# Second SwiGLU: up projections as seven block products, with weight sums formed in DRAM

## Chip, cores and metric

One Trainium2 chip, one core. The kernel is timed in device microseconds (us). It runs one decoder layer over 512 tokens. TensorE (PE) multiplies, VectorE (DVE) and ScalarE (ACT) do the elementwise work, GpSimd (POOL) a little of it, and SyncE (SP) issues the transfers.

## The reference, cut to what matters

```python
x = x + 0.5 * swiglu(rms_norm(x, ffn1_norm), ffn1_w_gate, ffn1_w_up, ffn1_w_down)
x = x + token_mixer(rms_norm(x, mix_norm), ...)
x = x + 0.5 * swiglu(rms_norm(x, ffn2_norm), ffn2_w_gate, ffn2_w_up, ffn2_w_down)
return rms_norm(x, final_norm)

def swiglu(x, w_gate, w_up, w_down):
    return (silu(x @ w_gate) * (x @ w_up)) @ w_down
```

x is 512 tokens by 1024 channels (D), the hidden width of each SwiGLU is 2816, and everything is float32. The change concerns `x @ w_gate` and `x @ w_up` of the second SwiGLU.

## The kernel before, in words

**Matmuls.** A float32 operand is split in a high part that TensorE's reduced float32 format holds (fp32r) and a low part, the rest. A product is then three matmuls into one PSUM bank: high weight by high operand, high by low, low by high (`mm3`, L548). The stationary block is 128x128 of weights; what streams is up to 512 columns, here tokens.

**Weights.** `stream` (L490 on) lists all weight blocks of the layer, in order of use, each 128x1024 floats (512 KB). `make` and `weights` (L520, L539) bring the next one: SP's load into a `raw` tile, a cast on ACT to `whi`, a subtraction on DVE to `wlo`. There are four tiles of each.

**Up projections.** The normalized x is turned so that channels lie on partitions; `operand` makes it one pair of tiles xh and xl of 128 x 8 x 512. The hidden width is 22 tiles of 128 (FT). For each, `ffn_up` (L705) takes a block for gate and one for up, makes 24 matmuls of 512 tokens for each (8 channel tiles by 3) into a `ps_gu` bank, and `gated` (L600) forms silu(gate) * up and splits it into hhi (ACT) and hlo (POOL).

**Down projections and output rows.** `rows` (L672) adds up all 8 output banks (4 tiles of 128 tokens by 2 halves of 512 channels, `ps_o`), hidden tile by hidden tile. The last three hidden tiles (TAIL) are done per token tile, so that token tile q is complete while the next is still being multiplied. The mixer's output projection goes through `rows` too, and calls `mixed` (L1111) for each complete token tile: x2 = sum + x, then `renorm` (L660). That one squares x2 (ACT), takes the root and the reciprocal (sb, 128x1), scales x2 to xn, has TensorE transpose xn into a `ps_xt` bank, and writes the two parts into the token columns q of xh and xl. In `channels` (L638), the first two blocks (SPLITS, L635) are multiplied in two pieces, 384 tokens (tiles 0 to 2) and then 128 (tile 3), so that TensorE can begin ahead of the last token tile.

**Order.** Every operation goes through a `Recorder` (L391), and a list scheduler, `Plan` (L146), puts all of them in one fixed order per engine by a cost for each (`cost`, L172) and by how many tiles are free. PSUM has 8 banks, tagged ps. Each engine works through its list in order, and waits on others where data demands it. Nearly all instructions are issued in one line (413, in the changed kernel 428), for they are recorded, so tiles tell what they are. The inputs are arranged on the host by `_layout`.

## Time and profile before

| | us |
|---|---|
| median of 3 runs | 1190.66 (1187.05 to 1193.71) |
| the profiled execution | 1187.19 |
| its span | 1185.4 |
| stage: first up projections | 19 to 250 |
| first down projections | 250 to 364 |
| token mixer | 364 to 766 |
| mixer's output rows | 766 to 813 |
| second up projections | 813 to 1057 |
| second down projections | 1057 to 1179 |

The span goes from the first to the last instruction of the profiled execution; its mean granted TensorE clock was 0.998 of full speed. The stages are read off the chain that ended last, in order of time, whose pieces name the PSUM tile that was being written. In a row of a timeline stand the start in us, the duration of one instruction, the engine, the line, the operation with its tiles (out<-in), the shapes, the count, and in brackets the idle time before it with what ended it. In a group's row stand the busy time in us, the mean ns of one, the idle time before them and its releasers. A row of windows gives the stretch and its length, busy time and instructions of PE, PEld (the load of stationary blocks), DVE, ACT and POOL, then the granted clock, the share of the DMA engines and GB/s.

### The profile page before, as it was taken

How to read it: one execution, taken by the hardware profiler on the slowest of the kernel's cores; microseconds unless marked ns; L12 is line 12 of the kernel's file. 1: busy time of each engine (PE TensorE's matmuls, PEld its weight loads, DVE VectorE, ACT ScalarE, POOL GpSimd, SP SyncE). 2: the span in 40 equal slices, each digit the busy share in tenths (PEclk: the TensorE clock that was granted, in tenths of full speed). 3: DMA queues.
4: the chain of work that ended last, by engine and by line, in shares of the span. 5: the costliest groups of instructions: out<-in, count | busy, mean ns of one | idle time of the engine just before them, and what ended most of it. 6: DMA issues, size and time to landing. Idle time of an engine off the chain costs nothing.

```text
span 1185.4 us, 14680 instructions
## 1 busy us (share of the span) xinstructions
PE 1159.8 (98%) x5944; PEld 951.9 (80%) x5944; DVE 543.4 (46%) x742; ACT 440.4 (37%) x712; POOL 164.2 (14%) x153
## 2 busy tenths in 40 slices
PE   9999999999999999999999999999999999999997
PEld 6888888888888777877777888888888888888886
DVE  7433333332227598985767532726223232322225
ACT  7332323222124865353656423325222232322113
POOL 4211111111100333241100000000111111110000
PEclk9999999999999999999999999999999999999999
DMA  8323222332234022211022232321223323223211
GB/s 310 123 89 133 89 100 96 101 111 92 95 101 142 22 103 100 96 55 54 1 64 80 89 124 89 93 103 72 95 101 107 107 89 106 90 94 102 89 54 71
DMA packets 36068, 113.64 MB, mean 96 GB/s; under 512 B 4128, under 2 KB 5152, under 8 KB 36000
## 3 DMA queue, kind: packets, MB, share of 16 engines
q1 hardware_dynamic: 36000, 112.70, 27.9%
q8 instruction: 46, 0.75, 0.3%
q14 instruction: 22, 0.18, 0.0%
HBM read 108.49 MB, written 4.19 MB: 95 GB/s over the span
## 4 chain that ended last, share of the span: by engine, by line
PE 88%; DVE 6%; ACT 3%; issue 1%; DMA 1%; SPq 0%; POOL 0%; ACTq 0%; DVEq 0%
PE ps_gu L413 40%; PE ps_o L413 23%; PE ps_in L413 16%; PE ps_ob L413 2%; PE ps_oa L413 2%; PE ps_f L413 1%; DVE root L413 1%; PE ps_s L413 1%; DVE xx L413 1%; DVE wlo L413 1%; PE ps_t L413 1%; PE ps_y L413 1%; PE ps_sum L413 0%; DMA raw<-in_gu_dram 0%; ACT sq L413 0%
## 5 line engine op out<-in xcount | busy, mean ns | idle before, releaser
L413 ACT CAST whi<-raw 128x1024 fp32r<-128x1024 f32 (+1 forms) x200 | 201.2, 1008 | 623.2 <-PE ps_gu L413 186.8
L413 DVE TENSOR_TENSOR wlo<-raw,whi 128x1024 fp32r<-128x1024 f32 (+1 forms) x200 | 242.6, 1217 | 359.2 <-ACT whi L413 346.2
L413 PE MATMUL ps_gu<-xh,whi 128*128 128x512 f32 (+1 forms) x720 | 277.5, 387 | 1.6 <-ACT whi L413 1.4
L413 PE MATMUL ps_gu<-xl,whi 128*128 128x512 f32 (+1 forms) x720 | 277.6, 387 | 0.6 <-DVE xl L413 0.5
L413 PE MATMUL ps_gu<-xh,wlo 128*128 128x512 f32 (+1 forms) x720 | 277.4, 386 | 0.0
L413 PEld LDWEIGHTS ps_gu<-xh,whi 128*128 128x128 f32 x720 | 135.3, 188 | 30.2 <-ACT whi L413 3.1
L413 PEld LDWEIGHTS ps_gu<-xl,whi 128*128 128x128 f32 x720 | 135.3, 188 | 28.4 <-DVE xl L413 1.7
L413 PEld LDWEIGHTS ps_gu<-xh,wlo 128*128 128x128 f32 x720 | 135.2, 188 | 26.8
L413 POOL TENSOR_TENSOR hlo<-gg,hhi 128x512 fp32r<-128x512 f32 x44 | 76.8, 1746 | 538.4 <-ACT hhi L413 529.2
L413 PE MATMUL ps_in<-xl,whi 128*128 128x512 f32 (+2 forms) x352 | 136.8, 389 | 1.2 <-DVE xl L413 1.2
L413 PE MATMUL ps_in<-xh,whi 128*128 128x512 f32 (+2 forms) x352 | 136.5, 388 | 0.9 <-ACT xh L413 0.9
L413 PE MATMUL ps_in<-xh,wlo 128*128 128x512 f32 (+2 forms) x352 | 136.6, 388 | 0.0
L413 PE MATMUL ps_o<-whi,hhi 128*128 128x512 f32 x352 | 113.7, 393 | 0.0
L413 PE MATMUL ps_o<-whi,hlo 128*128 128x512 f32 x352 | 113.6, 393 | 0.0
L413 PE MATMUL ps_o<-wlo,hhi 128*128 128x512 f32 x352 | 113.3, 392 | 0.0
L413 DVE TENSOR_TENSOR gg<-gg,ps_gu 128x512 f32<-128x512 f32 x44 | 30.2, 687 | 141.6 <-PE ps_gu L413 141.5
L413 PEld LDWEIGHTS ps_in<-xl,whi 128*128 128x128 f32 x352 | 66.7, 189 | 14.1 <-DVE xl L413 1.5
L413 PEld LDWEIGHTS ps_o<-wlo,hhi 128*128 128x128 f32 x352 | 66.2, 188 | 14.6
L413 PEld LDWEIGHTS ps_o<-whi,hlo 128*128 128x128 f32 x352 | 66.2, 188 | 14.6
L413 PEld LDWEIGHTS ps_in<-xh,whi 128*128 128x128 f32 x352 | 66.5, 189 | 14.1 <-ACT xh L413 1.2
L413 PEld LDWEIGHTS ps_o<-whi,hhi 128*128 128x128 f32 x352 | 66.1, 188 | 14.4
L413 PEld LDWEIGHTS ps_in<-xh,wlo 128*128 128x128 f32 x352 | 66.6, 189 | 12.7
(230 smaller groups left out, 1074.2 us busy)
## 6 DMA issues: line engine op xcount, KB each, us to landing
raw<-in_gu_dram SPq DMA_DIRECT2D x86, 512.0 KB, 3.4
raw<-in_dn_dram SPq DMA_DIRECT2D x44, 512.0 KB, 3.5
raw<-in_win_dram SPq DMA_DIRECT2D x42, 512.0 KB, 3.6
raw<-in_wo_dram SPq DMA_DIRECT2D x8, 512.0 KB, 3.4
x<-in_xT_dram SPq DMA_DIRECT2D x8, 256.0 KB, 4.3
xr<-in_x_dram SPq DMA_DIRECT2D x8, 256.0 KB, 6.2
x1d<-xr SPq DMA_DIRECT2D x8, 256.0 KB, 2.0
raw<-in_wout_dram SPq DMA_DIRECT2D x8, 256.0 KB, 2.5
```

Source lines behind the costliest of these rows:

```text
L413: return getattr(self.plan.engines[e], m)(**k)
```

## The change

**The algorithm.** The hidden tiles are taken in pairs, j = 0 to 10. Pair 0 is multiplied as before, except that all four of its blocks are done in the two pieces of 384 and 128 tokens (`2 * SPLITS`). For each pair j from 1 on, gate and up are each seen as a product of 2 x 2 blocks: two hidden tiles by two halves of D (KH = 4 channel tiles), and two halves of D by two halves of the tokens (256). Instead of eight block products there are seven, in the manner of Strassen and Winograd, on sums and differences of blocks. A block of `gu2` (now laid out as FJ x 4 x 128 x 1024) holds gate and up of one hidden tile and one half of D. A product is 4 x 3 matmuls of 256 columns for gate and as many for up (`block`), and accumulates in one of three pairs of banks, `ps_wx`, `ps_wc` and `ps_ww`. X is copied out between products (q1, u2 and u3, on ACT), and DVE adds the copies to the results. The hidden tile of the second kind comes out with its sign turned, which silu's scale of -1 and a factor of -1 undo.

**Sums of tokens.** Besides xh and xl, four combinations of token halves and halves of D are needed, as high and low parts: tf0 to tf3. `take`, called at the end of `renorm`, makes them from the transposed banks: token tiles 0 and 1 are kept (xt), and with tiles 2 and 3 come t1, t2 and two t34, each cut by `halve` into two casts (ACT) and two subtractions (DVE) of 128 x 2 x 128.

**Sums of weights.** For each pair four sums of blocks are needed: F1 = g2 + g3, F3 = g0 + g2, F2 = g0 + F1, F4 = g1 + F2. They are formed in DRAM, for two pairs at a time, by POOL's transfers of 128x2x1024 floats (1 MB), DRAM to DRAM: four copies, then four that accumulate. This makes 40 transfers. `step_sums` records one after each hidden tile of the first up projections but two (20), one after each row step of the first down projections (19) and one in the mixer's output rows. Each depends on the operation recorded just before it, so none is issued early. In the stream the blocks of a pair then come as g0, g1, F2, F3, F1, g3, F4.

**x2.** Its eight tiles no longer stay until the end: they are written to DRAM (x2d, by SP) in `mixed`, and read back as x3 for the last step.

**The planner** gets a cost for issuing a transfer on POOL (1500 ns), and a rate at which these are thought to land (SOFT).

```diff
+FJ = FT // 2
+KH = KT // 2
...
+    SOFT = 160.0
...
+        if method == "dma_start":
+            return 60.0 if eng == "SP" else 1500.0
...
-                if size:
+                if size and e == "POOL":
+                    soft = max(soft, now + 2000) + size / self.SOFT
+                    o.end = soft + 2000
+                elif size:
...
-    for ft in range(FT):
-        for gu in range(2):
-            stream.append((gu2[ft, :, gu * D:(gu + 1) * D], D))
+    sums = [Part(Slot(dram, [2, P, D], F32, "dram", f"sums{f}_{i}")) for f in range(4) for i in range(FJ // 2)]
+    def summed(f, j):
+        return sums[f * (FJ // 2) + (j - 1) // 2][(j - 1) % 2]
+    for j in range(FJ):
+        for b in range(4) if j == 0 else (0, 1, "F2", "F3", "F1", 3, "F4"):
+            stream.append((gu2[j, b] if isinstance(b, int) else summed(int(b[1]) - 1, j), D))
     for ft in range(FT):
         stream.append((dn2[ft], D))
+    def sum_steps():
+        for i in range(FJ // 2):
+            js = slice(1 + 2 * i, 3 + 2 * i)
+            f1, f2, f3, f4 = (sums[f * (FJ // 2) + i].rearrange("j p d -> p j d") for f in range(4))
+            for to, of in ((f1, 2), (f3, 0), (f2, 0), (f4, 1)):
+                yield G.dma_start(out=to, in_=gu2[js, of].rearrange("j p d -> p j d"))
+            for to, of in ((f1, 3), (f3, 2)):
+                yield G.dma_start(out=to, in_=gu2[js, of].rearrange("j p d -> p j d"), accum_op=ALU.add)
+            yield G.dma_start(out=f2, in_=f1, accum_op=ALU.add)
+            yield G.dma_start(out=f4, in_=f2, accum_op=ALU.add)
+    summing = sum_steps()
+    def step_sums():
+        op = next(summing, None)
+        if op:
+            op.deps.add(op.i - 1)
...
+            if ft > 1:
+                step_sums()
...
+                if gu is None:
+                    wk, wsl = w, sl(kt)
+                else:
+                    wk, wsl = w[kt // KH], slice(gu * S + kt % KH * P, gu * S + kt % KH * P + P)
+                mm3(ps[:, cs_], wk, x, wsl, cs_, kt == 0, kt == KT - 1)
...
-    def renorm(name, q, x3, gain, xg):
+    def renorm(name, q, x3, gain, xg, also=None):
...
+            if also:
+                also(q, hf, ps)
...
+            step_sums()
...
+    def halve(t, form, q):
+        for i in range(2):
+            hi, lo = (x[i][:, :, sl(q)].keyed(q) for x in form)
+            part = t.rearrange("p (k t) -> p k t", t=P)[:, 2 * i:2 * i + 2]
+            A.copy(out=hi, in_=part)
+            V.tensor_tensor(out=lo, in0=part, in1=hi.bitcast(F32), op=ALU.subtract)
...
+        def take(q, hf, ps):
+            flat = ps.rearrange("p k t -> p (k t)")
+            if q < 2:
+                t = t2k("xt")
+                A.copy(out=t, in_=flat)
+                kept[q, hf] = t
+                return
+            q -= 2
+            if hf == 0:
+                t1 = t2k("t1")
+                V.tensor_tensor(out=t1, in0=kept[q, 0], in1=flat, op=ALU.subtract)
+                halve(t1, forms[0], q)
+                kept[q] = t1
+                return
+            t2 = t2k("t2")
+            V.scalar_tensor_tensor(out=t2, in0=flat, scalar=-1.0, in1=kept[q], op0=ALU.mult, op1=ALU.subtract)
+            halve(t2, forms[1], q)
+            for i in range(2):
+                t = t2k("t34")
+                V.scalar_tensor_tensor(out=t, in0=t2, scalar=-1.0, in1=kept[q, i], op0=ALU.mult, op1=ALU.subtract)
+                halve(t, forms[2 + i], q)
...
+    def block(ps, w, gu, x, start):
+        for k in range(KH):
+            wsl = slice(gu * S + k * P, gu * S + (k + 1) * P)
+            whi, wlo = w
+            xhi, xlo = x(k)
+            T.matmul(ps, lhsT=whi[:, wsl], rhs=xhi, start=start and k == 0, stop=False, skip_group_check=True)
+            T.matmul(ps, lhsT=whi[:, wsl], rhs=xlo, start=False, stop=False, skip_group_check=True)
+            T.matmul(ps, lhsT=wlo[:, wsl], rhs=xhi, start=False, stop=k == KH - 1, skip_group_check=True)
...
+    def ffn_up(xg, forms):
+        split_left[0] = 2 * SPLITS
         hs = []
-        for ft in range(FT):
+        for cb in range(2):
+            ws = [weights(1), weights(1)]
             pair = [psum("ps_gu") for _ in range(2)]
             for gu in range(2):
-                channels(xg, pair[gu], weights())
+                channels(xg, pair[gu], ws, gu)
             hs.append(gated(pair, None))
+        H = 2 * P
+        def plain(kb, tb):
+            return lambda k: [t[:, kb * KH + k, tb * H:tb * H + H].keyed([(2 * tb, kb), (2 * tb + 1, kb)]) for t in xg]
+        def formed(i):
+            return lambda k: [t[k // 2][:, k % 2] for t in forms[i]]
+        for j in range(1, FJ):
+            def both(ps, x, start):
+                w = weights()
+                for gu in range(2):
+                    block(ps[gu], w, gu, x, start)
+            def aside(name):
+                t = t2k(name)
+                ps = [t[:, gu * H:gu * H + H].keyed(gu) for gu in range(2)]
+                for gu in range(2):
+                    A.copy(out=ps[gu], in_=X[gu])
+                return ps
+            X, C, W = ([psum(n)[:, 0:H] for _ in range(2)] for n in ("ps_wx", "ps_wc", "ps_ww"))
+            top = [t2k(n) for n in ("gg", "uu")]
+            low_ = [t2k(n) for n in ("gg", "uu")]
+            both(X, plain(0, 0), True)
+            q1 = aside("q1")
+            both(C, plain(1, 0), True)
+            for gu in range(2):
+                V.tensor_tensor(out=top[gu][:, 0:H].keyed(0), in0=C[gu], in1=q1[gu], op=ALU.add)
+            both(X, formed(1), False)
+            u2 = aside("u2")
+            both(X, formed(2), False)
+            u3 = aside("u3")
+            both(W, formed(0), True)
+            for gu in range(2):
+                V.tensor_tensor(out=low_[gu][:, H:S].keyed(1), in0=W[gu], in1=u3[gu], op=ALU.add)
+            both(X, formed(3), False)
+            A.activation(out=low_[0][:, 0:H].keyed(0), in_=X[0], func=AF.Silu, scale=-1.0)
+            A.copy(out=low_[1][:, 0:H].keyed(0), in_=X[1])
+            A.activation(out=low_[0][:, H:S].keyed(1), in_=low_[0][:, H:S].keyed(1), func=AF.Silu, scale=-1.0)
+            V.scalar_tensor_tensor(out=low_[0], in0=low_[0], scalar=-1.0, in1=low_[1], op0=ALU.mult, op1=ALU.mult)
+            both(W, plain(1, 1), False)
+            for gu in range(2):
+                V.tensor_tensor(out=top[gu][:, H:S].keyed(1), in0=W[gu], in1=u2[gu], op=ALU.add)
+            A.activation(out=top[0], in_=top[0], func=AF.Silu)
+            V.tensor_tensor(out=top[0], in0=top[0], in1=top[1], op=ALU.mult)
+            hs.append(finished(top[0]))
+            hs.append(finished(low_[0]))
...
+            Q.dma_start(out=x2d.keyed(2 * q + hf)[2 * q + hf], in_=x2)
+        renorm("sb", q, res[q], gain, xg, take)
...
-    o["gu2"] = gu(w["ffn2_w_gate"], w["ffn2_w_up"])
+    g2 = np.stack([w["ffn2_w_gate"], w["ffn2_w_up"]]).reshape(2, 2, KH, P, FJ, 2, P)
+    o["gu2"] = g2.transpose(4, 5, 1, 3, 0, 2, 6).reshape(FJ, 4, P, D)
```

**Where it moves instructions.** The first place is DVE between the mixer's output rows and the second up projections. sb2 and sb3 are the reciprocal roots of token tiles 2 and 3, xn their normalized tiles. Before, x2_5064 and x2_5076 are the two halves of token tile 3, and the first row is the second xn of token tile 2:

```order
L413 SCALAR_TENSOR_TENSOR xn_6429<-x2_5046,sb2_6384,gff2_4948 128x512
L413 TENSOR_TENSOR x2_5064<-ps_o_6158,x2_5064 128x512
L413 TENSOR_TENSOR wlo_6446<-raw_6212,whi_6431 128x1024
L413 TENSOR_TENSOR xl_6365<-ps_xt_6434,xh_6358 128x4x128
L413 TENSOR_TENSOR xl_6365<-ps_xt_6441,xh_6358 128x4x128
L413 TENSOR_TENSOR x2_5076<-ps_o_6160,x2_5076 128x512
L413 TENSOR_TENSOR wlo_6475<-raw_6242,whi_6461 128x1024
L413 TENSOR_TENSOR sb3_6451<-sb3_6451 128x1
L413 TENSOR_TENSOR wlo_6487<-raw_6272,whi_6468 128x1024
L413 RECIPROCAL sb3_6451<-sb3_6451 128x1
L413 SCALAR_TENSOR_TENSOR xn_6503<-x2_5064,sb3_6451,gff2_4930 128x512
L413 SCALAR_TENSOR_TENSOR xn_6508<-x2_5076,sb3_6451,gff2_4948 128x512
```

In the changed kernel x2_5123 and x2_5135 are the halves of token tile 3, xt the kept tiles 0 and 1:

```order
L428 TENSOR_TENSOR sb2_6450<-sb2_6450 128x1
L428 TENSOR_TENSOR x2_5135<-ps_o_6219,x2_5135 128x512
L428 RECIPROCAL sb2_6450<-sb2_6450 128x1
L428 SCALAR_TENSOR_TENSOR xn_6516<-x2_5099,sb2_6450,gff2_4989 128x512
L428 SCALAR_TENSOR_TENSOR xn_6522<-x2_5105,sb2_6450,gff2_5007 128x512
L428 TENSOR_TENSOR sb3_6504<-sb3_6504 128x1
L428 TENSOR_TENSOR wlo_6530<-raw_6272,whi_6511 128x1024
L428 TENSOR_TENSOR xl_6434<-ps_xt_6524,xh_6422 128x4x128
L428 TENSOR_TENSOR t1_6553<-xt_6429,ps_xt_6524 128x512
```

A few rows further on, still in the changed kernel, the last sums of this token tile and the start of token tile 3's:

```order
L428 SCALAR_TENSOR_TENSOR t34_6579<-t2_6568,xt_6429 128x512
L428 TENSOR_TENSOR tf1l_6587<-t2_6568,tf1h_6576 128x2x128
L428 TENSOR_TENSOR tf1l_6593<-t2_6568,tf1h_6582 128x2x128
L428 TENSOR_TENSOR tf2l_6599<-t34_6579,tf2h_6590 128x2x128
L428 TENSOR_TENSOR tf2l_6603<-t34_6579,tf2h_6595 128x2x128
L428 SCALAR_TENSOR_TENSOR t34_6606<-t2_6568,xt_6438 128x512
L428 RECIPROCAL sb3_6504<-sb3_6504 128x1
L428 TENSOR_TENSOR wlo_6613<-raw_6302,whi_6520 128x1024
L428 TENSOR_TENSOR tf3l_6626<-t34_6606,tf3h_6616 128x2x128
L428 TENSOR_TENSOR tf3l_6632<-t34_6606,tf3h_6619 128x2x128
L428 SCALAR_TENSOR_TENSOR xn_6636<-x2_5123,sb3_6504,gff2_4989 128x512
L428 SCALAR_TENSOR_TENSOR xn_6642<-x2_5135,sb3_6504,gff2_5007 128x512
```

Before, the reciprocal and the xn of token tile 2 stood ahead of tile 3's x2; now they stand behind the last of it. Between token tile 2's xn and token tile 3's now stand two wlo, two xl, the four sums t1, t2 and t34, and eight halves of tf0 to tf3 (two of each of them at this place).

The second place is POOL in the mixer, where bh is the product that the mixer's key step needs. Before:

```order
L412 MEMSET xx_2301 64x4x64
L412 MEMSET xx_2331 64x4x64
L413 TENSOR_TENSOR bh_2841<-iclr_2764,ilam_2829 128x512
L413 TENSOR_TENSOR bh_2853<-iclr_2777,ilam_2845 128x512
L413 TENSOR_TENSOR bh_2864<-iclr_2812,ilam_2856 128x512
L413 TENSOR_TENSOR bh_2878<-iclr_2823,ilam_2867 128x512
```

Now (sums0 to sums3 are F1 to F4, and the last number of the name the two pairs):

```order
L428 DMA sums1_4_2351<-in_gu2_dram 128x2x1024
L427 MEMSET xx_2362 64x4x64
L427 MEMSET xx_2381 64x4x64
L428 DMA sums3_4_2387<-in_gu2_dram 128x2x1024
L428 DMA sums0_3_1998<-in_gu2_dram 128x2x1024
L428 DMA sums2_3_2034<-in_gu2_dram 128x2x1024
L428 DMA sums3_2_1841<-sums1_2_1754 128x2x1024
L428 TENSOR_TENSOR bh_2895<-iclr_2817,ilam_2882 128x512
L428 TENSOR_TENSOR bh_2907<-iclr_2830,ilam_2899 128x512
```

34 of the 40 transfers now stand ahead of the first bh. The last of them, sums3_2<-sums1_2, accumulates the F2 of its pairs, and so it waits for that one's landing, which is the 27th transfer in POOL's order.

More of the change, by code (lines that the diff above doesn't have):

```diff
@@ L130, in __init__ @@
         self.users, self.state, self.made, self.place, self.held = [], {}, None, None, {}
-        self.psum = tag == "ps"
+        self.psum, self.dram = tag == "ps", tag == "dram"
     def real(self):
         if self.made is None:
-            self.made = self.pool.tile(list(self.shape), self.dt, tag=f"{self.tag}{self.place}" if self.tag else self.name, name=self.name)
+            self.made = self.pool.tile(list(self.shape), self.dt, tag=f"{self.tag}{self.place}" if self.place is not None else self.name, name=self.name)
         return self.made
@@ L199, in add @@
         op = Op()
-        op.port = sum(isinstance(p.tile, Slot) and not p.tile.psum and p.free > 1 for p in parts)
+        op.port = sum(isinstance(p.tile, Slot) and not p.tile.psum and not p.tile.dram and p.free > 1 for p in parts)
         op.i, op.ways, op.table, op.outs = len(self.ops), ways, table, []
@@ L253, in order @@
         free_at = {e: 0.0 for e in names}
-        table, dma, dge, port = None, 0.0, 0.0, 0.0
+        table, dma, dge, soft, port = None, 0.0, 0.0, 0.0, 0.0
         front, now, done = 0, 0.0, 0
@@ L407, in record @@
                     size = 4 * int(np.prod((out if isinstance(out, Part) else kw["in_"]).arr.shape))
+                    if isinstance(out, Part) and out.tile.dram:
+                        size *= 2
                 def emit(e=e, m=m):
@@ L636, in layer_kernel, with channels @@
     split_left = [0]
-    def channels(xg, ps, w):
+    def channels(xg, ps, w, gu=None):
         cols = [(0, NQ)]
@@ L647, in channels @@
                 x = [t[:, kt].keyed([(q, kt // 4) for q in range(a, b)]) for t in xg]
-                mm3(ps[:, cs_], w, x, sl(kt), cs_, kt == 0, kt == KT - 1)
+                if gu is None:
[3 more added lines that the diff above has]
+                mm3(ps[:, cs_], wk, x, wsl, cs_, kt == 0, kt == KT - 1)
     def rstd_of(name, x3):
@@ L703, in halves, with token_sums, tiles @@
         return out_
-    def ffn_up(xg):
-        split_left[0] = SPLITS
+    def halve(t, form, q):
[4 more added lines that the diff above has]
+            V.tensor_tensor(out=lo, in0=part, in1=hi.bitcast(F32), op=ALU.subtract)
+    def token_sums():
+        def tiles(name, where):
+            if where is None:
+                return [t2k(name, [P, 2, 2 * P], F32R) for _ in range(2)]
+            t = Part(Slot(inv, [P, KH, 2 * P], F32R, "inv", name))
+            return [t[:, 0:2], t[:, 2:4]]
+        forms = [[tiles(f"tf{i}{part}", inv if i == 0 else None) for part in "hl"] for i in range(4)]
+        kept = {}
+        def take(q, hf, ps):
[19 more added lines that the diff above has]
+                halve(t, forms[2 + i], q)
+        return forms, take
@@ L707, in ffn_up, with finished @@
+    def finished(gg):
+        hi = t2k("hhi", dt=F32R)
+        lo = t2k("hlo", dt=F32R)
+        A.copy(out=hi, in_=gg)
+        G.tensor_tensor(out=lo, in0=gg, in1=hi.bitcast(F32), op=ALU.subtract)
+        return hi, lo
+    def ffn_up(xg, forms):
+        split_left[0] = 2 * SPLITS
         hs = []
-        for ft in range(FT):
+        for cb in range(2):
+            ws = [weights(1), weights(1)]
             pair = [psum("ps_gu") for _ in range(2)]
             for gu in range(2):
-                channels(xg, pair[gu], weights())
+                channels(xg, pair[gu], ws, gu)
@@ L749, in layer_kernel @@
     xg = operand()
-    x1d = Part(Slot(dram, [2 * NQ, P, S], F32, None, "x1d"))
+    x1d = Part(Slot(dram, [2 * NQ, P, S], F32, "dram", "x1d"))
     def first_done(q, ps):
@@ L1109, in layer_kernel @@
     xg = operand()
+    x2d = Part(Slot(dram, [2 * NQ, P, S], F32, "dram", "x2d"))
+    forms, take = token_sums()
     def mixed(q, ps):
@@ L1114, in mixed @@
             V.tensor_tensor(out=x2, in0=ps[hf], in1=x2, op=ALU.add)
-        renorm("sb", q, res[q], gain, xg)
+            Q.dma_start(out=x2d.keyed(2 * q + hf)[2 * q + hf], in_=x2)
+        renorm("sb", q, res[q], gain, xg, take)
     rows(ms, mixed)
-    hs = ffn_up(xg)
+    hs = ffn_up(xg, forms)
     gain = halves("gfin", gfin)
+    res = []
+    for q in range(NQ):
+        res.append([])
+        for hf in range(2):
+            t_ = t2k("x3")
+            Q.dma_start(out=t_, in_=x2d.keyed(2 * q + hf)[2 * q + hf])
+            res[q].append(t_)
     def last(q, ps):
```

## Prediction

> **What bounds the kernel now.** I read the page first: the share of each engine, then the chain that ended last.
>
> ```profile
> span 1185.4 us, 14680 instructions
> ...
> PE 1159.8 (98%) x5944; PEld 951.9 (80%) x5944; DVE 543.4 (46%) x742; ACT 440.4 (37%) x712; POOL 164.2 (14%) x153
> ...
> PE 88%; DVE 6%; ACT 3%; issue 1%; DMA 1%; SPq 0%; POOL 0%; ACTq 0%; DVEq 0%
> ```
>
> TensorE is the bound nearly everywhere, and DVE, ACT and POOL have room. So the change is worth what it takes off TensorE, less every place where TensorE has to stand. Next I read the chain of waits in order of time where the second feed-forward runs:
>
> ```profile
> 813.90 4.80 PE ps_gu L413 x26
> 819.76 237.22 PE ps_gu L413 x1075
> 1056.98 121.52 PE ps_o L413 x528
> ```
>
> From 813.9 to 1057.0 the chain never leaves TensorE: no load, cast or subtraction holds it, and the down projection follows without a gap. Only the up projections are rewritten, so only these 243 us can shrink. The pace inside them is best read from POOL's timeline, where one subtraction (hlo) ends each tile of 128 hidden channels:
>
> ```profile
> 840.90 1.78 POOL L413 TENSOR_TENSOR hlo<-gg,hhi 128x512 fp32r<-128x512 f32 x1 [9.05 <-ACT hhi L413]
> ...
> 1058.63 1.65 POOL L413 TENSOR_TENSOR hlo<-gg,hhi 128x512 fp32r<-128x512 f32 x1 [9.20 <-ACT hhi L413]
> ```
>
> They are the second and the last of 22, so 20 tiles lie between: 217.73 / 20 = 10.89 us for 48 matmuls of 512 columns, 226.8 ns each.
>
> **Part 1, the matmuls.** For two tiles of hidden channels the old code needs 96 matmuls of 512 columns, the new one 7 products x 2 (gate, up) x 4 x 3 = 168 of 256 columns: in columns 7/8, in instructions 7/4. So the price of a 256-column matmul decides, and this trace has none. It has 384 and 128 columns, in the two blocks that are split by token columns; TensorE's timeline, starts in us:
>
> ```profile
> 815.25 0.33 PE L413 MATMUL ps_gu<-xh,wlo 128*128 128x384 f32 x1
> ...
> 817.85 0.33 PE L413 MATMUL ps_gu<-xh,wlo 128*128 128x384 f32 x1
> ...
> 825.68 0.27 PE L413 MATMUL ps_gu<-xl,whi 128*128 128x128 f32 x1
> ...
> 828.14 0.28 PE L413 MATMUL ps_gu<-xh,wlo 128*128 128x128 f32 x1
> ```
>
> The first two are 15 matmuls apart: 173.3 ns for 384 columns. The last two are 22 apart: 111.8 ns for 128. From 384 to 512 columns the price rises 0.418 ns a column, and that line leaves 12.8 ns per matmul which does not depend on width; it would give 66 ns at 128, so there something else, of 111.8 ns, sets the pace: the load of the stationary block, one for each matmul. At 256 columns the line gives 119.8 ns, just above this floor. The floor bounds it below, 111.8 ns. Above, the straight chord from 128 to 384 columns bounds it: 142.6 ns. I take the line, plus a little, because four of the seven products stream operands out of the small shared tiles, not out of the one big operand. What that does is seen in two pieces of the chain:
>
> ```profile
> 700.32 43.55 PE ps_in L413 x192
> 743.87 22.24 PE ps_ob L413 x96
> ```
>
> The first streams the big operand, 226.8 ns; the second small tiles, 231.7 ns. Half of the 4.9 ns for 4 of 7 products is 1.4 ns: 121 ns.
>
> Before, 42 unsplit blocks x 24 x 226.8 ns = 228.6 us. Now two of these become split ones, each 24 x (173.3 + 111.8) ns = 6.84 us, together 13.7 us; the other 40 become 1680 matmuls x 121 ns = 203.3 us. Sum -11.6 us. The bounds give -27.1 us (111.8 ns) and +24.7 us (142.6 ns); the work breaks even at 127.9 ns.
>
> The Trainium skill speaks to this price (TensorE: Matmul & The Clock Gate, Back-to-back issue gap): a warm matmul of N columns takes N/2.4 + 2.5 ns, by estimate 109.2 ns at 256 columns and 215.8 ns at 512; this trace does not agree, with 226.8 ns at 512. By that estimate the sum of this part would be -31.5 us, and the rows, which hold 111.8 ns even at 128 columns, decide against it.
>
> **Part 2, the start of the up projections.** The new code makes four more operand forms from the normalized tokens, on DVE and ACT, between the last output product of the mixer and the first up projection. Both orders of DVE stand above, with the change. What the operations cost is in the groups with each shape apart, and in DVE's timeline:
>
> ```profile
> L413 DVE TENSOR_TENSOR wlo<-raw,whi 128x1024 fp32r<-128x1024 f32 x184 | 234.1, 1275 | 353.3 <-ACT whi L413 346.0
> L413 ACT CAST whi<-raw 128x1024 fp32r<-128x1024 f32 x184 | 193.3, 1052 | 611.4 <-PE ps_gu L413 186.8 <-PE ps_o L413 182.0 <-issue 145.1
> ...
> L413 DVE TENSOR_TENSOR wlo<-raw,whi 128x256 fp32r<-128x256 f32 x8 | 3.1, 416 | 0.2 <-ACT whi L413 0.2
> ...
> L413 ACT COPY rhs<-ps_x 128x256 f32<-128x256 f32 x8 | 2.6, 375 | 0.9 <-PE ps_x L413 0.9
> ```
> ```profile
> 814.36 0.68 DVE L413 TENSOR_TENSOR x<-ps_o,x 128x512 f32<-128x512 f32 x1
> ...
> 817.29 0.15 DVE L413 RECIPROCAL sb<-sb 128x1 f32<-128x1 f32 x1
> 817.48 1.41 DVE L413 SCALAR_TENSOR_TENSOR xn<-x,sb,gff 128x512 f32<-128x512 f32 x2
> ```
>
> TensorE waits today for almost none of it; its own timeline:
>
> ```profile
> 813.90 0.45 PE L413 MATMUL ps_gu<-xl,whi 128*128 128x384 f32 x1 [0.49 <-DVE xl L413]
> ```
>
> Now token tile 2 is normalized only after the sum of tile 3 (x2, then the reciprocal, then xn), so behind the end E of the last output product come 0.17 us of signal, 0.68, 0.15 and 0.70 us until its transposes can start, then a cast and a subtraction: TensorE starts the up projection at about E + 3.6 us. Before, it stood 0.5 us there, and its transposes lay among the output products (0.7 us that only move): 2.5 us more. Second, between tile 2's xn and tile 3's, DVE now has 2 wlo (2 x 1.28 us), 2 xl and 4 sums over 512 elements (6 x 0.68), and 8 halves (8 x 0.42): 10.0 us. Tile 2's xn end at E + 2.4, so tile 3's first one ends at about E + 13.1. TensorE's cover is 45 matmuls x 173.3 ns = 7.8 us, to E + 11.4; 1.7 us and one more short wait make 1.9 us. Bounds for both: 0.5 us (the waits of today) and 7 us (no cover from the second split pair). Third, the clock. After the same renormalization ahead of the mixer it drops; the row of that stretch (its third column from the right is the granted clock), and TensorE's timeline in it:
>
> ```profile
> 364.00:382.00 18.00, 15.90 (x77) 13.57 (x76) 14.92 (x26) 9.80 (x22) 0.00 (x0) 0.91 0.48 158
> ```
> ```profile
> 378.08 0.53 PE L413 MATMUL ps_in<-xl,whi 128*128 128x384 f32 x1
> ...
> 380.96 0.52 PE L413 MATMUL ps_in<-xl,whi 128*128 128x384 f32 x1
> ```
>
> Nine starts in 2.88 us are 320 ns each instead of 173: behind 2.1 us of TensorE idleness (18.00 - 15.90), ten matmuls lost 1.5 us. With some 3 us idle at the new start I charge the same 1.5 us (0 to 1.7, one such stretch at half pace). The Trainium skill (TensorE: Matmul & The Clock Gate, Part 1: The HAM clock gate) says that half clock follows an idle window of about 3.4 us; this trace shows it behind 2.1 us, in pieces. By the Trainium skill this term would be nil, and the sum 1.5 us better.
>
> **Part 3, the other work of a step.** One j (two tiles) lasts 168 x 121 ns = 20.3 us. ACT has 7 casts and six copies of 128x256 out of PSUM, DVE 7 subtractions and a few sums. By the rows of part 2 the seven are 7.4 and 8.9 us, the rest some 5 and 4: about 12.5 us on each engine, under 20.3. The tight spot is the third product: bank X is copied out (u2) and at once written again. Gate and up halves alternate, so each copy has 12 matmuls, 1.45 us, to hide 0.38 us and two signals, and the ACT order puts at most one cast of 1.05 us in front: it fits, barely. I charge 0.5 us over ten steps (0 to 10 x 0.6 us, if each step were late by half a cast). The stream now brings 512 KB per 2.9 us.
>
> **Part 4, the sums in DRAM.** POOL issues 40 transfers of 1 MB, the first behind the third hlo, and in the mixer its products (bh) stand behind 34 of them; the last of those waits for the landing of the 27th. POOL's timeline, the issues by kind and the queue:
>
> ```profile
> 44.53 1.79 POOL L413 TENSOR_TENSOR hlo<-gg,hhi 128x512 fp32r<-128x512 f32 x1 [2.40 <-ACT hhi L413]
> ...
> 403.21 5.04 POOL L413 TENSOR_TENSOR bh<-iclr,ilam 128x512 f32<-128x512 f32 x4 [87.13 <-ACT ilam L413]
> ```
> ```profile
> raw<-in_gu_dram SPq DMA_DIRECT2D x86, 512.0 KB, 3.4
> ...
> x1d<-xr SPq DMA_DIRECT2D x8, 256.0 KB, 2.0
> ```
> ```profile
> q1 hardware_dynamic: 36000, 112.70, 27.9%
> ```
>
> 27 landings between 46.3 and 403.2 us allow 13.2 us for each. No row shows such a transfer. Lower bound: 112.70 MB in 27.9% of 1185.4 us is 341 GB/s, 3.1 us for 1 MB counted once. Upper bound: read and write at the landing times of the rows, 2 x 3.4 + 4 x 2.0 = 14.8 us, and 6.8 us more where the target is read too: 18.2 us on average. Queued transfers go by rate, so I count read, write and target at 341 GB/s: 6.2 and 9.2 us, mean 7.7 us, and 11 us with the weights taking 30% of the engines. That is under 13.2, so no wait. Cost: two issues among the key products, 0.7 us (0, in POOL's gaps, to 3.6, two hlo lengths). The write and reload of x2 and the loads behind it on SP's queue I cost at nothing: five blocks are loaded ahead.
>
> **Sum**, against the profiled execution's 1187.19 us (span 1185.4 and 1.8 around it): -11.6 + 2.5 + 1.9 + 1.5 + 0.5 + 0.7 = -4.5 us. The median, 1190.66 us, lies 3.5 us above that execution; on it the forecast is **1186.2 us**.
>
> **The rivals.** (a) *Half the columns, half the price.* If the 12.8 ns belong to the switch between PSUM banks of 512 columns and not to each matmul, 256 columns cost 113.4 ns: 1680 x 7.6 ns = 12.8 us better, 1173.4 us. For it: 113.4 is above the floor. Against: 384 columns pay them too. The Trainium skill's 2.5 ns, above, makes the same claim. (b) *POOL blocked, slower.* If a transfer takes longer than 13.2 us on average, POOL stands in front of bh by 27 times the excess; DVE's in-order queue waits for bh with the wlo of the next weights behind it, and TensorE runs dry after three prepared blocks (16 us). It decides from 13.8 us on; at 15 us it costs 48.6 - 16 = 32 us: 1219 us. For it: the upper bound, and accumulating must read its target. Against: the rate. (c) *Loads of the stationary block collide with matmuls of nearly equal length*: 131.6 ns, halfway to the chord, is 17.8 us worse, 1204 us. Against: 111.8 ns were kept with far shorter matmuls. (d) *Weights late*: 512 KB in 2.9 us is 181 GB/s, just over half of 341, four buffers deep; unlikely, some 20 us.
>
> **How the numbers follow.** Forecast 0.62, with a range of its own of 1179 to 1193; (a) 0.14, (b) 0.13, (c) 0.08, (d) 0.03. A measurement of this kernel tells about 0.5% from no change, 6 us: 1184.7 to 1196.6. The forecast's 4.5 us lie inside that and near its edge: 0.23 faster, 0.37 same, 0.02 slower. With (a) faster, (b) slower but for 0.01, (c) and (d) slower: faster 0.37, same 0.38, slower 0.25. The range 1172 to 1204 leaves out most of (b) and the outer ends of (a) and (c), under 2 in 10.
>
> **What would show it.** Right: starts of ps_wx, ps_wc and ps_ww 121 ns apart; two waits of TensorE ahead of ps_gu (about 3 and 2 us) and a dip of the clock there; no idleness within a step; bh on POOL near 403 us with ACT as its releaser. Wrong: bh released by a transfer and late (b); a pace under 115 or over 128 ns (a, c); waits of ps_w tiles on whi or on a load (d).

## The result, and the profile after

| | before | after |
|---|---|---|
| median of 13 runs each, us | 1189.39 | 1182.71 |
| ratio after to before, 95% interval | | 0.9939 [0.9922, 0.9957] |
| the profiled execution, us | 1187.19 | 1180.79 |
| first down projections' end to output rows (mixer) | 402.08 | 407.84 |
| output rows to the end of the second up projections | 290.87 | 278.42 |

The changed kernel is 6.7 us faster by the medians, where 4.5 us were forecast. All times here are of executions in the chip's faster state; one of the six of early_one, below, ran at a mean granted clock of 0.616, took 1718.13 us and is left out. The page of the profile after, its span and its engines:

```profile
span 1179.0 us, 16693 instructions
...
PE 1150.9 (98%) x6712; PEld 978.5 (83%) x6712; DVE 617.6 (52%) x862; ACT 500.8 (42%) x839; POOL 189.9 (16%) x190
```

TensorE is as full as before, only with less to do. The shares hide where the time went; the chain in order of time shows it. First two pieces of the kernel before, start and length in us, that the prediction did not need:

```profile
364.03 3.94 PE ps_o L413 x17
...
766.11 36.65 PE ps_o L413 x159
```

And the chain of the changed kernel:

```profile
364.66 3.93 PE ps_o L428 x17
...
772.50 36.58 PE ps_o L428 x159
...
822.59 7.90 PE ps_gu L428 x44
...
850.41 2.93 PE ps_wx L428 x24
853.33 2.88 PE ps_wc L428 x24
...
1050.92 121.81 PE ps_o L428 x528
```

Taking the two executions apart at these pieces: up to 364 us the new one is 0.63 us later. From there to the output rows it takes 407.84 instead of 402.08 us, 5.76 us **lost**. From the output rows to the second down projections it takes 278.42 instead of 290.87 us, 12.45 us **won**. The rest is 0.34 us shorter. Together -6.40 us, the difference of the two profiled executions. So the up projections gained more than twice what I had reckoned, and the mixer, whose code did not change, gave nearly half of it back.

**The up projections.** The stretch of the ten steps, in the row of windows:

```profile
850.40:1050.90 200.50, 200.50 (x1682) 200.50 (x1681) 125.94 (x150) 116.21 (x189) 28.52 (x19) 1.00 0.60 197
```

TensorE does not stand for one moment, at full clock. From the first ps_wx to the down projections there are 200.5 us for 1680 matmuls: 119.3 ns each. DVE works 63% of the stretch and ACT 58%; 197 GB/s are moved, and no engine's wait in this stretch ends with a load. Then TensorE's timeline at the start:

```profile
820.21 1.22 PE L428 MATMUL ps_xt<-cs,xn 128*128 128x128 f32 x8 [1.73 <-ACT sq L428]
821.56 0.96 PE L428 MATMUL ps_gu<-xh,whi 128*128 128x384 f32 x4
822.59 0.44 PE L428 MATMUL ps_gu<-xl,whi 128*128 128x384 f32 x1
...
832.83 0.22 PE L428 MATMUL ps_gu<-xl,whi 128*128 128x128 f32 x1
```

One wait of 1.73 us, as forecast: tile 2's xn stand behind the x2 of tile 3. The bracket names ACT, but in DVE's timeline these xn start at 819.32 us, right behind that x2 and the reciprocal, and the transposes follow at 820.21. The second wait, for token tile 3, is not there: the pieces of 384 tokens go on up to 832.8, 14.5 us behind the end E of the last output product (818.3 us), because eight of the second pair's follow those of the first before the pieces of token tile 3 go on.

**POOL.** POOL's timeline with the last transfer ahead of bh, and bh; then the page's issues by kind, whose last column is the median time to landing:

```profile
341.47 1.13 POOL L428 DMA_DIRECT2D sums<-sums  x1 [7.98 <-issue]
402.29 5.04 POOL L428 TENSOR_TENSOR bh<-iclr,ilam 128x512 f32<-128x512 f32 x4 [59.69 <-ACT ilam L428]
```

```profile
sums<-in_gu_dram POOLq DMA_DIRECT2D x30, 1024.0 KB, 8.3
...
sums<-sums POOLq DMA_DIRECT2D x10, 1024.0 KB, 9.5
```

POOL has issued the last of them 60 us before bh, and stands then for ACT's ilam, as before. From issue to landing they take 8.3 and 9.5 us in the median, where 13.2 us were left for each.

**The mixer.** What is new in its waits is in the list of TensorE's waits between 458 and 535 us, of before and of after:

```profile
PE ps_i L413 <- DVE un L413: 1.4, 1, 1.4
```
```profile
PE ps_i L428 <- DVE un L428: 3.0, 1, 3.0
```

un is a transpose on DVE that ps_i needs. Behind the longer wait the granted clock (third column from the right) falls for 10 us; windows of the changed kernel:

```profile
500.00:502.00 2.00, 0.10 (x1) 0.00 (x0) 2.00 (x2) 0.80 (x4) 0.73 (x3) 1.00 0.00 0
...
504.00:506.00 2.00, 2.00 (x6) 1.50 (x5) 1.93 (x6) 1.51 (x7) 1.83 (x2) 0.50 0.00 0
...
510.00:512.00 2.00, 2.00 (x49) 1.28 (x46) 0.00 (x0) 1.32 (x5) 0.00 (x0) 0.50 1.08 215
```

These windows point at what the loss consists of, and the windows of the whole mixer settle it for the two executions, first before, then after:

```profile
364.03:766.11 402.08, 386.63 (x2505) 314.03 (x2505) 273.40 (x433) 203.91 (x393) 64.85 (x78) 1.00 0.24 79
```
```profile
364.66:772.50 407.84, 392.34 (x2505) 316.68 (x2505) 275.89 (x439) 202.90 (x390) 67.21 (x81) 0.98 0.33 93
```

TensorE stands idle for 15.45 us in the one and 15.50 us in the other. Of the 5.76 us, 5.71 are busy time of the same 2505 matmuls. So in these two executions the longer wait for un is made up elsewhere, and what is lost is clock: in windows of 2 us it lies under 1.00 before the change from 376 to 382 us only, and after it from 410 to 414, 502 to 514 and 620 to 626 us. Busy time times the missing share of the clock, added up over these windows, is 1.7 us before and 7.9 us after (an estimate from the rows). The profiled execution of before had a mean clock of 0.998, near the top of its executions (0.987 to 0.999 in the 28 beside early), so part of the 5.76 us can be its luck; the experiments ask what remains in the medians.

The mixer's code is the same, but its order is not. Six of POOL's transfers stand in it, each costed at 1500 ns by the planner, which lays out everything anew around them: between the last ps_t and the first ps_i it puts 167 matmuls of the input projection (ps_in) where it put 236 before.

### The profile page after: what moved, and what is told of

Its sections match the earlier page's. It is cut to its first block, busy times and chain, and to the rows that moved or that the text cites. A ratio compares the mean times of both kernels' runs of the same rounds, so it can differ in the third digit from the quotient of the medians.

```text
span 1179.0 us, 16693 instructions
## 1 busy us (share of the span) xinstructions
PE 1150.9 (98%) x6712; PEld 978.5 (83%) x6712; DVE 617.6 (52%) x862; ACT 500.8 (42%) x839; POOL 189.9 (16%) x190
## 4 chain that ended last, share of the span: by engine, by line
PE 89%; DVE 5%; ACT 4%; issue 1%; DMA 1%; SPq 0%; DVEq 0%; ACTq 0%
PE ps_o L428 24%; PE ps_gu L428 22%; PE ps_in L428 16%; PE ps_wx L428 10%; PE ps_ww L428 5%; PE ps_wc L428 2%; PE ps_ob L428 2%; PE ps_oa L428 2%; PE ps_f L428 1%; DVE root L428 1%; PE ps_s L428 1%; PE ps_t L428 1%; DVE wlo L428 1%; PE ps_y L428 1%; PE ps_pq L428 1%
## 5 line engine op out<-in xcount | busy, mean ns | idle before, releaser
L428 ACT CAST whi<-raw 128x1024 fp32r<-128x1024 f32 (+1 forms) x230 | 232.6, 1013 | 547.0 <-PE ps_o L428 179.0
L428 DVE TENSOR_TENSOR wlo<-raw,whi 128x1024 fp32r<-128x1024 f32 (+1 forms) x230 | 274.9, 1198 | 342.0 <-ACT whi L428 334.8
L428 PE MATMUL ps_gu<-xh,whi 128*128 128x512 f32 (+2 forms) x416 | 155.6, 377 | 3.4 <-ACT whi L428 3.0
L428 PE MATMUL ps_gu<-xl,whi 128*128 128x512 f32 (+2 forms) x416 | 156.4, 377 | 0.2
L428 PE MATMUL ps_gu<-xh,wlo 128*128 128x512 f32 (+2 forms) x416 | 156.1, 377 | 0.0
L428 POOL TENSOR_TENSOR hlo<-gg,hhi 128x512 fp32r<-128x512 f32 x44 | 70.7, 1608 | 517.2 <-ACT hhi L428 509.2
L428 PE MATMUL ps_o<-wlo,hhi 128*128 128x512 f32 x352 | 113.4, 392 | 0.0
L428 PEld LDWEIGHTS ps_gu<-xh,whi 128*128 128x128 f32 x416 | 78.0, 188 | 19.1 <-ACT whi L428 4.3
L428 PEld LDWEIGHTS ps_gu<-xl,whi 128*128 128x128 f32 x416 | 78.2, 188 | 15.1 <-DVE xl L428 1.3
L428 PEld LDWEIGHTS ps_gu<-xh,wlo 128*128 128x128 f32 x416 | 78.2, 188 | 13.5
L428 PEld LDWEIGHTS ps_in<-xl,whi 128*128 128x128 f32 x352 | 66.9, 190 | 14.4 <-DVE xl L428 1.5
L428 PEld LDWEIGHTS ps_in<-xh,whi 128*128 128x128 f32 x352 | 66.8, 190 | 14.4 <-ACT xh L428 1.2
L428 PEld LDWEIGHTS ps_o<-whi,hhi 128*128 128x128 f32 x352 | 66.0, 188 | 14.5
L428 DVE TENSOR_TENSOR gg<-gg,ps_gu 128x512 f32<-128x512 f32 x24 | 16.4, 687 | 67.7 <-PE ps_gu L428 67.6
```

The costliest lines, as they stand in the source:

```text
L428: return getattr(self.plan.engines[e], m)(**k)
```

## The experiments

Theory 1: the mixer's loss comes from the planner's order, and in particular from the wait for un and the clock behind it. Theory 2: it comes from the transfers themselves. Theory 3: it is the chance of one execution. All results; the mixer, and TensorE's idle time in it, are measured in the profiled execution, by the same two pieces of the chain as above. Each ratio is to executions of the kernel before that ran beside that experiment, with medians from 1188.4 to 1189.4 us:

| kernel | median us | ratio to before | mixer us | TensorE idle in it, us |
|---|---|---|---|---|
| before | 1189.4 | | 402.08 | 15.45 |
| after | 1182.7 | 0.9939 [0.9922, 0.9957] | 407.84 | 15.50 |
| early | 1178.4 | 0.9902 [0.9873, 0.9931] | 402.61 | 15.88 |
| tiny_sums | 1181.9 | 0.9932 [0.9912, 0.9952] | 411.18 | 15.54 |
| before_sums | 1194.1 | 1.0035 [1.0016, 1.0053] | 407.63 | 15.55 |
| keep_warm | 1182.7 | 0.9940 [0.9919, 0.9961] | 413.47 | 15.59 |
| slow_un | 1191.6 | 1.0017 [1.0001, 1.0033] | 410.99 | 17.29 |
| before_256 | 1199.8 | 1.0076 [1.0046, 1.0106] | 404.08 | 15.83 |
| no_sums | 1177.2 | 0.9897 [0.9873, 0.9921] | 402.82 | 16.02 |
| early_one | 1176.0 | 0.9883 [0.9860, 0.9906] | 403.57 | 15.14 |
| soft_180 | 1176.6 | 0.9894 [0.9863, 0.9924] | 405.44 | 15.02 |
| soft_200 | 1177.1 | 0.9900 [0.9870, 0.9931] | 402.08 | 14.50 |

The profiled executions of tiny_sums, keep_warm and slow_un were 3 to 5 us above their medians and that of soft_200 2.4 us below, so a single mixer time can be off by as much. The idle time is nearly the same in all but slow_un: what differs between the mixers here is mostly TensorE's pace.

### early: all transfers ahead of the mixer

```diff
-    SOFT = 160.0
+    SOFT = 300.0
```

> The planner is told that POOL's transfers land nearly twice as fast (SOFT 300 instead of 160), so that 39 of the 40 stand ahead of bh instead of 34; TensorE's and DVE's orders in the mixer are then those of the kernel before. Theory 1 (order): the mixer's extra 5.7 us (402.1 before, 407.9 after) come from the order that the planner made around the six transfers that stood in it: TensorE stood 3.0 us in one piece ahead of un, and the clock went to 0.5 for 10 us. Then the mixer takes 402 us, the clock stays at 1.00 there, and the time falls from 1182.7 to about 1177 us, 0.990 of before. Theory 2 (traffic: the six issues and their bytes in the mixer delay it): also about 402 us here. Theory 3 (chance of one execution): mixer unchanged near 408 or scattered, 1182 us. If a transfer takes longer than the 9.1 us that are left for each (39 landings from 47 to 402 us), POOL stands ahead of bh and the mixer gets longer by up to 39 times the excess.

The mixer took 402.61 us and the ratio is 0.9902, as theories 1 and 2 said. Its chain and POOL's bh:

```profile
365.98 3.95 PE ps_o L428 x17
...
768.59 36.65 PE ps_o L428 x159
```
```profile
387.57 1.15 POOL L428 DMA_DIRECT2D sums<-sums  x1 [10.11 <-PE ps_in L428]
403.65 5.05 POOL L428 TENSOR_TENSOR bh<-iclr,ilam 128x512 f32<-128x512 f32 x4 [14.94 <-issue]
```

bh comes 37.7 us behind the first piece, 39.2 us before the change: even with 39 transfers ahead POOL is on time. The clock was not at 1.00 throughout, which I had expected it to be: 0.93 and 0.64 stand in the windows from 408 to 412 and to 416 us, where the changed kernel has a dip as well.

### tiny_sums: the same order, next to no bytes

```diff
+TINY = 8
...
-            f1, f2, f3, f4 = (sums[f * (FJ // 2) + i].rearrange("j p d -> p j d") for f in range(4))
+            f1, f2, f3, f4 = (sums[f * (FJ // 2) + i].rearrange("j p d -> p j d")[:, :, 0:TINY] for f in range(4))
```

> The planner's order is that of the changed kernel, but each of POOL's 40 transfers carries 8 floats a row instead of 1024 (8 KB instead of 1 MB), and the stream takes plain blocks in place of the sums: what is left out are the sums of weights, so the hidden tiles come out with other numbers, while every instruction of the other engines stays. Theory 1 (order): mixer 408 us as in the changed kernel, with the 3.0 us wait ahead of un and the half clock behind it; 1182 us. Theory 2 (traffic): mixer back to about 402 us, 1177 us. Both: second up projections unchanged at 232 us.

```profile
364.12 3.95 PE ps_o L431 x17
...
775.30 36.58 PE ps_o L431 x159
```
```profile
PE ps_i L431 <- DVE un L431: 3.0, 1, 3.0
```

Its chain and its wait, above: with 1/128 of the bytes in the changed kernel's order the loss is all there: 1181.9 us, the wait of 3.0 us too. The bytes of theory 2 fall; the issues on POOL are still in this order, and soft_180 and soft_200, below, speak to them.

### before_sums: the transfers alone, in the kernel before

```diff
+            if ft > 1:
+                step_sums()
...
+            step_sums()
```

(with `sum_steps` and the planner's costs of the changed kernel, reading `gu2` as it lay before; nobody reads the sums)

> The kernel before with the 40 transfers of 1 MB added at the same places, their results never read. The planner then gives the mixer the order of the changed kernel. Theory 1 and theory 2: mixer 408 instead of 402 us and the second up projections unchanged at 244 us, so 5 to 6 us slower than before, ratio 1.005. Theory 3: ratio 1.000. If the transfers slowed the first feed-forward too (its weights come through the same DMA engines), its 345 us from first to last matmul would grow; I expect no growth.

```profile
364.57 3.94 PE ps_o L421 x17
...
772.20 36.58 PE ps_o L421 x159
```

1.0035, some 4 us slower by the ratio and 5 by the medians, and a mixer of 407.63 us: the price of the transfers' place in the order without any of the gain. The loss comes in a third program with this order, in its median too, so theory 3 falls. From the first to the last matmul of the first feed-forward nothing grew: its up projections had 221.93 us in the piece of 979 matmuls, as before.

### keep_warm: two matmuls that fill the wait for un

```diff
+        ps = psum("ps_keep")
+        for _ in range(KEEP):
+            T.matmul(ps, lhsT=one, rhs=uo.rearrange("p s i -> p (s i)")[:, 0:S], start=True, stop=True)
```

> The changed kernel with two matmuls of 512 float32 columns added, which read uo and whose result nobody uses; they stand where TensorE waited 3.0 us for un, and cover some 1.7 us of it. Nothing else of the computation changes. Theory 1, its second half (it is the clock that costs, not the wait): the wait is cut in two of under 1.5 us, the clock stays at 1.00 in this stretch, and the mixer takes about 4 us less, 404 us; the time about 1179 us. If the wait alone costs, and the clock is no matter: mixer still about 408 us, as the added matmuls end before un does.

```profile
502.35 2.81 PE L429 MATMUL ps_keep<-uo,one 128*128 128x512 f32 x4 [2.27 <-DVE uo L429]
```
```profile
504.00:506.00 2.00, 2.00 (x19) 0.82 (x17) 1.93 (x6) 1.94 (x8) 1.66 (x3) 0.50 0.00 0
506.00:508.00 2.00, 1.52 (x25) 0.91 (x21) 1.87 (x7) 0.53 (x3) 0.00 (x0) 0.82 0.00 0
508.00:510.00 2.00, 2.00 (x24) 1.33 (x22) 1.29 (x5) 1.90 (x5) 0.00 (x0) 1.00 0.00 0
```

A miss. The low clock lasted some 3.5 us instead of 10, yet the median is that of the changed kernel. The 2.27 us ahead of the filler were enough to lower the clock, and the filler itself took 2.81 us of TensorE, much of it at that clock. What was saved went into it, so this run's median doesn't tell clock and wait apart. Its mixer of 413.47 us also holds the filler and another dip, of half clock from 636 to 650 us, far behind it.

### slow_un: the wait lengthened in the kernel before

```diff
+        for _ in range(SLOW):
+            wait = t2k("wait")
+            op = V.tensor_tensor(out=wait, in0=wi.rearrange("p i j -> p (i j)")[:, 0:S], in1=wi.rearrange("p i j -> p (i j)")[:, S:2 * S], op=ALU.add)
+            op.ways = {"DVE": (0.0,) + op.ways["DVE"][1:]}
```

> The kernel before with three additions of 128x512 on DVE put between uo and un, whose results nobody reads; the planner is told that they cost nothing, so TensorE's order up to the wait is that of before. The wait ahead of un grows from 1.4 to about 3.3 us. Theory 1, its second half (a wait of some 3 us lets the clock fall to 0.5, and that costs more than the wait): mixer 1.9 us longer by the wait and up to 5 us more by the clock, 406 to 409 us instead of 402; 0.5 in the clock's column behind un. If the wait alone costs: 404 us, and the clock stays at 1.00.

```profile
PE ps_i L414 <- DVE un L414: 3.5, 1, 3.5
```
```profile
516.00:518.00 2.00, 0.00 (x0) 0.00 (x0) 2.00 (x2) 0.93 (x5) 1.87 (x7) 0.94 0.00 0
518.00:520.00 2.00, 1.84 (x70) 1.84 (x71) 1.86 (x10) 0.00 (x0) 0.00 (x0) 0.50 0.03 8
...
522.00:524.00 2.00, 2.00 (x56) 1.31 (x52) 1.94 (x6) 1.53 (x7) 1.17 (x2) 1.00 0.00 0
```

The wait grew to 3.5 us and the clock did fall, but for about 3.4 us only, and the median rose by 2 us, about the wait itself. So the second half of theory 1, as I had put it, falls for the order of before: a wait of this length at this place does not make 5 us there. The 410.99 us of the profiled mixer are 1.84 us of added idle time, and the rest is clock, most of it in a dip from 632 to 648 us, far behind un.

### soft_180 and soft_200: other orders, transfers still in the mixer

```diff
-    SOFT = 160.0
+    SOFT = 180.0
```

> The changed kernel with SOFT 180 instead of 160: 37 transfers stand ahead of bh and three still in the mixer behind it, and the planner puts 250 matmuls of the mixer's input projection ahead of the first that needs un (167 in the changed kernel, 236 before). If it is the order that costs, and not transfers in the mixer: the wait ahead of un is at most 1.5 us, the mixer takes 402 to 404 us, and the time is that of the early transfers, 1178 us (ratio 0.990). If transfers in the mixer cost as such, three of the six are left: 1180 to 1181 us.

> The changed kernel with SOFT 200: again three transfers in the mixer, and 215 matmuls ahead of the first that needs un, between the changed kernel's 167 and the 236 of before. By the order: a wait ahead of un of 1.5 to 3 us and a mixer of 402 to 408 us, 1178 to 1182 us. By the transfers as such: the same as with SOFT 180.

Both have three full transfers in the mixer and both are as fast as early. The waits ahead of un are not short; TensorE's waits of soft_180, and then of soft_200:

```profile
PE ps_i L428 <- DVE un L428: 2.0, 1, 2.0
```
```profile
PE ps_i L428 <- DVE un L428: 2.4, 1, 2.4
```

So transfers in the mixer cost nothing as such that shows: by theory 2 the three that are left would have meant 1180 to 1181 us. The order costs, in the changed kernel by 4 to 6 us of the medians.

How it does so is settled for the profiled executions only. The low clock behind un lasts 10 us in all three whose order brings the wait of 3.0 us (after, tiny_sums, before_sums), 7 us in soft_180 and soft_200, and 3.4 us or nothing in the others, keep_warm and slow_un among them. So soft_200 doesn't clear the wait: its mixer pays some 3 us for that clock too and comes out at 402.08 us with no other dip, where before has the one at 376 us, and with 0.95 us less idle time. Whether these dips carry the loss in the medians too is open. The other executions have only a mean clock over the span, and at the same 0.993 two of the changed kernel took 1182.18 and 1182.71 us, one of early 1178.60. Which of the moved instructions matter was not settled.

### no_sums: no transfers at all

```diff
-        for b in range(4) if j == 0 else (0, 1, "F2", "F3", "F1", 3, "F4"):
+        for b in range(4) if j == 0 else (0, 1, 0, 0, 2, 3, 1):
...
-        op = next(summing, None)
+        op = None
```

> The changed kernel without POOL's 40 transfers; the stream takes plain blocks in place of the sums, so what is left out are the sums of weights, and the hidden tiles come out with other numbers. The mixer's order is that of before. If the transfers cost nothing where they do not change the order: the same time as with the early transfers, 1178 us, ratio 0.990. If 42 MB more in the first feed-forward and mixer cost something by themselves, this kernel is faster than that by as much.

0.9897 against 0.9902: within the intervals, 42 MB of transfers for the sums cost nothing that can be measured once they do not disturb the order.

### before_256: the width alone

```diff
-        cols = [(0, NQ)]
+        cols = [(0, NQ // 2), (NQ // 2, NQ)] if two else [(0, NQ)]
```

> The kernel before with all blocks of the second up projections multiplied in two pieces of 256 tokens: no products are saved, no sums, only the width changes. If the 119.3 ns of the changed kernel belong to the width, its 44 blocks take 44 x 48 x 119.3 ns = 252.0 us instead of 42 x 24 x 226.8 ns + 2 x 6.84 us = 242.3 us: 9.7 us slower, ratio 1.008. If the small operand tiles or the many banks of the changed kernel make its matmuls dearer or cheaper, the pace here differs from 119.3 ns: at 113.4 ns the stage would be 2.8 us shorter than before, at 127.9 ns 28 us longer.

```profile
821.85 247.43 PE ps_gu L413 x2062
```

247.43 us for 2062 matmuls are 120.0 ns each, and the kernel is 0.76% slower than before. The pace belongs to the width: in the changed kernel it is 120 ns too where the big operand streams (2.88 us for 24 ps_wc, above), and a little less where the small tiles do, or the mean would not be 119.3 ns. Halving the width costs 5.8% of TensorE's time in these products; the eighth of the products that is saved, less this, is the gain.

### early_one: only the first pair split

```diff
-    SOFT = 160.0
+    SOFT = 300.0
...
-        split_left[0] = 2 * SPLITS
+        split_left[0] = SPLITS
```

> The early transfers, and only the first pair's two blocks multiplied in the pieces of 384 and 128 tokens, as before the change, instead of the first four. That saves 2 x 24 x (285.1 - 226.8) ns = 2.8 us of matmuls. My second wait (1.9 us for token tile 3) was reckoned with the cover of the first pair alone; the trace showed that the split second pair gave more cover, and the wait did not come. Without that cover TensorE should stand for token tile 3 for 1 to 3 us, in the order of what is saved: time within 0.2% of the early transfers, 1176 to 1180 us.

TensorE's idle stretches between 812 and 850 us are two:

```profile
815.86 1.23 PE L428 MATMUL ps_xt<-cs,xn 128*128 128x128 f32 x8 [1.73 <-ACT sq L428]
...
818.24 0.59 PE L428 MATMUL ps_gu<-xl,whi 128*128 128x384 f32 x1 [0.43 <-DVE xl L428]
```

Nothing waits for token tile 3 here either, where I had expected 1 to 3 us: a miss. But the clock was at 0.57 from 818 to 822 us, and the 44 matmuls of the start took 9.46 us instead of the changed kernel's 7.90; without these 1.6 us the transposes of tile 3 would have been due about when its xn was done. So the run doesn't show that the second split gives no needed cover. From the output rows to the down projections it has 278.20 us where early has 280.05. At 1176.0 us it is among the fastest kernels here, 1.2% below before, with early, soft_180 and soft_200 too close to be told apart from it.

## Why the prediction was right, and where its terms were off

The direction, the mechanism and the range held: 1186.2 us forecast, 1182.7 measured; the 0.61% that the kernel is faster lie just above the 0.5% named there, where I had put the forecast just inside. Of the 3.5 us between forecast and measurement 1.3 are the base: the median of before was 1190.66 us in three executions and is 1189.39 in 13. The sum was -4.5 us, against -6.4 us between the two profiled executions. Term by term:

- **The matmuls, -11.6 us.** 121 ns were put in, 119.3 ns measured: 200.5 instead of 203.3 us, so -14.4 us. The line through 384 and 512 columns gave 119.8 ns at 256, and that line was right. The addition for small operand tiles was wrong: they are no dearer here.
- **The first wait, +2.5 us.** The start came 3.2 us behind the last output product, by the row of 1.73 us and eight transposes, where I had 3.6. TensorE stands 1.73 us there instead of 0.49.
- **The second wait, +1.9 us.** It did not come. The failed step is "TensorE's cover is 45 matmuls x 173.3 ns": the first pair has 48, and I gave no weight to the 384-column pieces of the second pair, eight of which TensorE does before it needs tile 3's last parts. DVE was earlier too: in its timeline the two xn of tile 3 start at 829.33 us, so the first ends near E + 11.7 instead of E + 13.1.
- **The clock, +1.5 us.** Not in this execution. Of the eight programs with the new start, four show a dip behind it in their profile (early, tiny_sums, no_sums, early_one) and four do not, so as a mean it is about half of what I charged (9.46 us against 7.90 for the same 44 matmuls, 1.6 us where it falls).
- **Stalls within a step, +0.5 us.** None: busy 200.50 of 200.50 us.
- **The mixer, +0.7 us.** 5.8 us in its place, and this is the step that really failed: "two issues among the key products". I priced what POOL's transfers hold up on POOL. What cost was the planner, which wrote a different order for every engine of the mixer around them; in the profiled execution TensorE did the same matmuls in that order with the same idle time, but 5.71 us slower, at a lower clock. I had both orders and looked for it at bh alone.

Of the rivals, (a) gave 113.4 ns and (c) 131.6 (halfway from 121 to 142.6 would be 131.8); the rows show 119.3 and 120.0. (b), POOL blocked, was ruled out by a landing in 8.3 to 9.5 us where the bound was 13.2, and in early by 39 transfers in time. (d), weights late: no wait for a load in the ten steps. The two large errors, 7.2 us too dear in the up projections and 5.1 us too cheap in the mixer, stood against each other, and that the sum is so near is partly luck.

## What to carry to other kernels

Half the width at half the price is nearly true here, where the line from two measured widths gave 119.8 ns at 256 columns and the price at 128 columns was 111.8, so a fast product of seven instead of eight can pay even when it halves the columns. A background transfer that costs nothing on any engine can still cost some 5 us through a list scheduler, as here: compare the order of every engine where they stand, and try two or three values of a planner's constant before judging a change. Price cover by what stands in TensorE's order next, not by the tile that the code names.

## What the runs showed of the hardware

**The same wait lowers the clock or doesn't.** ps_sum waits 2.1 us for hi in both kernels; the idle time in brackets, then the windows behind it, first of the kernel before:

```profile
409.70 0.50 PE L413 MATMUL ps_sum<-hi,blk_r 128*128 128x512 f32 x1 [2.06 <-DVE hi L413]
```
```profile
410.00:414.00 4.00, 3.95 (x17) 2.93 (x16) 4.00 (x4) 3.97 (x6) 3.55 (x3) 1.00 0.01 2
```

And of the kernel after:

```profile
408.77 0.51 PE L428 MATMUL ps_sum<-hi,blk_r 128*128 128x512 f32 x1 [2.09 <-DVE hi L428]
```
```profile
410.00:414.00 4.00, 4.00 (x11) 2.81 (x11) 4.00 (x4) 3.97 (x6) 3.80 (x3) 0.57 0.22 42
```

By the windows of 2 us the dips last 3.4 us (slow_un behind un), 6.8 us (soft_180 and soft_200), 10.2 us (un, above) or 13.6 us, in one execution of slow_un from 632 us on, where no wait over 0.8 us stands in the 10 us ahead:

```profile
632.00:636.00 4.00, 4.00 (x38) 3.28 (x38) 3.18 (x9) 1.86 (x6) 0.00 (x0) 0.73 0.19 71
...
640.00:644.00 4.00, 4.00 (x33) 3.06 (x32) 0.00 (x0) 1.30 (x5) 0.00 (x0) 0.50 0.00 0
644.00:648.00 4.00, 4.00 (x21) 3.55 (x22) 1.87 (x4) 1.93 (x6) 0.33 (x1) 0.57 0.00 0
```

The Trainium skill (TensorE: Matmul & The Clock Gate, Part 1: The HAM clock gate) describes a free-running window of about 3.4 us by which the clock is set; the lengths, and that a 2 us wait counts in one execution and not in another, agree with a grid of that kind. By that page the array turns cold after a whole idle window; the rows show that 2.1 us can be enough. So executions of one kernel differ in their clock: of the 28 of the kernel before that ran beside early, one took 1187.11 us at a mean clock of 0.999 and one 1197.04 us at 0.987. That the clock alone makes this difference is not shown, for no run here changed the clock alone.
